# A decoder block in fp32: the up-projection by seven block products in place of eight, activations through DRAM

## The chip, the cores and the metric

The kernel runs on one core of a Trainium2 chip, as one program. The metric is the device time of one execution in microseconds (us). TensorE (PE) multiplies, VectorE (DVE), ScalarE (ACT) and GpSimd (POOL) work elementwise, SyncE (SP) issues the transfers between DRAM and SBUF. Accumulators stand in PSUM, eight banks of 128 x 512 fp32.

## The reference, cut to what matters

SEQ is 1024, D_MODEL 1024, D_FF 2816. The whole block is computed: modulation rows from c, two attention branches, their merge and w_out, the feed-forward part, a last norm. The part that the change touches:

```python
def conv_ffn(h, w_up, conv_w, conv_b, w_down):
    u = h @ w_up                                   # [1024, 2 * 2816]
    up = jnp.pad(u, ((0, 0), (CONV_WIDTH - 1, 0), (0, 0)))
    u = conv_b + sum(conv_w[j] * up[:, j:j + s] for j in range(CONV_WIDTH))
    gate, val = u[..., :D_FF], u[..., D_FF:]
    return (jax.nn.silu(gate) * val) @ w_down
...
    x = x + g_m[:, None, :] * mix                  # mix: the branches merged, times w_out
    h = modulate(rmsnorm(x, norm_ffn_g[l]), sh_f, sc_f)
    x = x + g_f[:, None, :] * conv_ffn(h, ...)
return rmsnorm(x, norm_final_g)
```

## The kernel before, in words

Every fp32 operand of a matmul is split into a high part (`hi_act`, a copy on ScalarE into the type fp32r, L75) and a low part (the operand minus its high part, `lo_dve` on VectorE, L84, or `lo_pool` on GpSimd, L87). One product of 128 x 128 by 128 x 512 is then three matmuls: high by high, high by low, low by high (`mm3`, L94 to L96).

The phases run one after the other: modulated input and projections, attention with the gate projections as fillers, then `mix_and_up`, `ffn_up` and `ffn_down`. A scheduler sets the order of instructions on each engine from the order of the code and the data that each needs; the loads go through one queue on SP, in order. Buffers come from pools: a name (tag) with a number of buffers that are used in turn, and whoever asks for the next one waits for the last reader of the old contents.

`mix_and_up` merges the branches (L962 to L975), then multiplies by w_out in four groups: two halves of the tokens times two halves of 512 columns, each with four accumulators. `load` and `scaled_rows` bring rows of w_out, scaled by the modulation row gm on GpSimd (L1069). `residual` adds x (L1001), `modulated` makes the norm of a token tile (L1009 on VectorE, L1010 on VectorE or for three tiles on GpSimd). The rows gm, gf and sf are made by `late_row` in the merging loop, each by a load of partial sums, a split, and four matmuls. `by_feature` transposes the normalised tiles on TensorE and splits them: h2[c], eight blocks of 128 features by 512 tokens, for two token chunks c.

`ffn_up` takes 22 blocks j of 128 columns, each with its gate columns and its value columns. `columns_of` loads 128 columns (512 KB, into a buffer of `wr`, a tag with two buffers) and splits them in halves by `halves`: high parts on ScalarE, low parts on GpSimd. Each block needs four accumulators (gate and value, two chunks) of 8 x 3 matmuls, 96 in all. `conv` reads the accumulators in PSUM: ScalarE makes the first tap with the bias (L1090), VectorE adds the other two (L1096), and short pieces of one or two tokens come from the earlier chunk. `gated` takes the sigmoid on ScalarE (L1105), multiplies by it on GpSimd (L1106) and by the value on VectorE (L1109). The 22 results stay in SBUF as `acts`.

`ffn_down` makes two passes of 512 columns over all 22 blocks, eight accumulators each: `split_act` splits an activation block, `scaled_rows` brings w_down scaled by a gain row. It loads the residual rows x2 in its first steps.

## Time and profile before

| what | value |
|---|---|
| time, median of 3 runs | 1697.14 us (1696.16 to 1700.38) |
| profiled execution: span from the first to the last instruction | 1692.6 us |
| the median's distance to this span | 4.5 us |
| matmuls in the profile | 7966 |
| ScalarE busy | 679.5 us (40%) |
| bytes moved by DMA | 197.74 MB, mean 117 GB/s |
| rows of w_up, loads | 44 of 512 KB |

The profiled execution has no time of its own beside its span; the runs were timed apart from it. A busy share is the time in which an engine had an instruction under way; a matmul's duration is longer than the distance between two starts, since matmuls are pipelined. "Idle before" is the time that an engine stood before instructions of a group, with what ended it.

### The profile page before, as it was taken

To read this page: it belongs to the slowest core of one execution; us is meant where nothing else is said; L and a number is where in the kernel's file an instruction comes from. 1 tells how busy PE (TensorE), PEld (TensorE's weight loads), DVE (VectorE), ACT (ScalarE), POOL (GpSimd) and SP (SyncE) were. 2 spreads that over 40 slices of the span, in tenths; PEclk is the share of its full clock that TensorE was granted. 3 is DMA by queue.
4 is the path that set the end of the run, shared out by engine and by line. 5 is a ranking of instruction groups with operands and counts; after the bars stand their busy time and mean duration, and the time that the engine had idled before them with its cause. 6 is when DMAs were issued, how large, how long until landed. Compare 5 with 4: busy or idle time off the path is not lost.

```text
span 1692.6 us, 21545 instructions
## 1 busy us (share of the span) xinstructions
PE 1640.9 (97%) x7966; PEld 1349.1 (80%) x7966; DVE 911.7 (54%) x1620; ACT 679.5 (40%) x1265; POOL 597.5 (35%) x490
## 2 busy tenths in 40 slices
PE   7999989999989999999999899999999999999997
...
PEclk9999999999989999999999999999999999999999
...
GB/s 291 128 113 165 176 257 194 201 201 180 153 179 86 119 123 99 108 127 268 126 99 175 106 50 50 50 50 51 50 51 49 41 48 64 154 50 38 50 50 100
DMA packets 160696, 197.74 MB, mean 117 GB/s; under 512 B 9698, under 2 KB 106658, under 8 KB 159246
## 3 DMA queue, kind: packets, MB, share of 16 engines
...
## 4 chain that ended last, share of the span: by engine, by line
PE 53%; DVE 3%; ACT 1%; DMA 1%; issue 0%; SPq 0%; ACTq 0%
PE ps_mm L95 17%; PE ps_mm L96 17%; PE ps_mm L94 17%; PE ps_tr L314 0%; DVE h2x_h L1009 0%; DMA o_raw<-dram_gate 0%; DMA o_raw<-dram_o 0%; DVE h2x_h L1010 0%; PE psA_pt L767 0%; DVE small_rstd L106 0%; PE psA_pt L96 0%; PE psA_pt L94 0%; PE psA_pt L95 0%; PE psA_s L738 0%; PE psA_o L779 0%
## 5 line engine op out<-in xcount | busy, mean ns | idle before, releaser
L87 POOL TENSOR_TENSOR ws_wl<-wr_wr,ws_wh 128x512 fp32r<-128x512 f32 x150 | 200.5, 1338 | 390.5 <-ACT ws_wh L75 351.2
L94 PE MATMUL ps_mm<-h_h,ws_wh 128*128 128x512 f32 x704 | 274.6, 390 | 0.0
L95 PE MATMUL ps_mm<-h_h,ws_wh 128*128 128x512 f32 x704 | 274.5, 390 | 0.0
L96 PE MATMUL ps_mm<-h_h,ws_wl 128*128 128x512 f32 x704 | 274.4, 390 | 0.0
L75 ACT ACTIVATE ws_wh<-wr_wr 128x512 fp32r<-128x512 f32 x226 | 142.1, 631 | 250.8 <-PE ps_mm L95 146.6
L1096 DVE SCALAR_TENSOR_TENSOR up_uv<-ps_mm,cw_cw,up_uv 128x511 f32<-128x511 f32 (+1 forms) x132 | 69.5, 568 | 163.8 <-ACT up_uv L1090 163.0
L95 PEld LDWEIGHTS ps_mm<-h_h,ws_wh 128*128 128x128 f32 x704 | 132.4, 188 | 27.9 <-DVE h_h L84 0.4
L96 PEld LDWEIGHTS ps_mm<-h_h,ws_wl 128*128 128x128 f32 x704 | 132.4, 188 | 27.5
L94 PEld LDWEIGHTS ps_mm<-h_h,ws_wh 128*128 128x128 f32 x704 | 132.4, 188 | 27.4
L94 PE MATMUL psA_fill<-hT_hi,ws_wh 128*128 128x512 f32 x352 | 150.0, 426 | 0.0
L96 PE MATMUL psA_fill<-hT_hi,ws_wl 128*128 128x512 f32 x352 | 139.4, 396 | 0.0
L95 PE MATMUL psA_fill<-hT_lo,ws_wh 128*128 128x512 f32 x352 | 139.3, 396 | 0.0
L1096 DVE SCALAR_TENSOR_TENSOR act_act<-ps_mm,cw_cw,act_act 128x511 f32<-128x511 f32 (+1 forms) x132 | 69.4, 568 | 122.2 <-ACT act_act L1090 121.4
L748 ACT ACTIVATE att_p<-psA_s,small_soft 128x128 f32<-128x128 f32 (+7 forms) x128 | 94.8, 740 | 99.9 <-DVE small_soft L742 98.4
L738 PE MATMUL psA_s<-opn_k,opn_q 96*128 96x256 f32 (+7 forms) x480 | 115.0, 360 | 13.8 <-DMA opn_k<-opn_stg 7.9
L742 DVE TENSOR_REDUCE small_soft<-psA_s 128x1 f32<-128x128 f32 (+7 forms) x128 | 96.0, 752 | 52.8 <-PE psA_s L740 52.4
L1106 POOL TENSOR_TENSOR act_act<-act_act,up_sg 128x512 f32<-128x512 f32 x44 | 56.7, 1289 | 158.9 <-ACT up_sg L1105 158.9
L84 DVE TENSOR_TENSOR ws_wl<-wr_wr,ws_wh 128x512 fp32r<-128x512 f32 x76 | 84.4, 1113 | 32.7 <-ACT ws_wh L75 32.5
L95 PE MATMUL ps_mm<-ws_wl,ahp_ah 128*128 128x512 f32 x256 | 101.5, 396 | 0.0
L94 PE MATMUL ps_mm<-ws_wh,ahp_ah 128*128 128x512 f32 x256 | 101.3, 396 | 0.0
L738 PEld LDWEIGHTS psA_s<-opn_k,opn_q 96*128 96x128 f32 (+1 forms) x480 | 82.5, 193 | 23.0 <-issue 13.4
L96 PE MATMUL ps_mm<-ws_wh,ahp_al 128*128 128x512 f32 x256 | 100.5, 393 | 0.0
...
## 6 DMA issues: line engine op xcount, KB each, us to landing
...
```

Source lines behind the costliest of these rows:

```text
L75: self.nc.scalar.activation(out, in_, AF.Copy, scale=scale)
L84: self.nc.vector.tensor_tensor(out=out, in0=in_, in1=f32(hi), op=ALU.subtract)
L87: self.nc.gpsimd.tensor_tensor(out=out, in0=in_, in1=f32(hi), op=ALU.subtract)
L94: mm(ps, lhsT=lh, rhs=rh, start=start, stop=False)
L95: mm(ps, lhsT=lh, rhs=rl, start=False, stop=False)
L96: mm(ps, lhsT=ll, rhs=rh, start=False, stop=stop)
L738: mm(o, lhsT=l, rhs=r[:, keys], start=n_ == 0, stop=diag is None and n_ == len(passes) - 1)
L742: nc.vector.tensor_reduce(out=st[:, 0:1], in_=view(s), axis=AX.X if i < 4 else AX.XY, op=ALU.max, negate=True)
L748: nc.scalar.activation(po, view(s), AF.Exp, bias=st[:, 0:1], accum_out=st[:, 1:2])
L1096: nc.vector.scalar_tensor_tensor(out=d, in0=src, scalar=cw[:, tap, jj : jj + 1], in1=d, op0=ALU.mult, op1=ALU.add)
L1106: nc.gpsimd.tensor_tensor(out=act, in0=act, in1=sg, op=ALU.mult)
```

## The change

**Seven products.** The feature axis (1024 = two halves of 512) and the token axis (two chunks of 512) of the right-hand side are taken as four blocks B11, B12, B21, B22; the gate and value columns of block j as A11, A12 (gate) and A21, A22 (value). Winograd's form of Strassen's scheme needs seven products of 4 x 3 matmuls: `product` with A11 B11, A12 B21, s1 N1, s2 T2, s3 N3, s4 B22 and A22 N4. The sums of weights s1 to s4 are made by four additions on VectorE for each block (`sums`, L1157 to L1160), and split; the sums of the right-hand side (N1, T2, N3, N4) are made once, in `second_chunk`, by token tile. B11 and B21 come from `first_chunk`. Three products are accumulated onto a bank that already holds another one, whose first value has been copied out (c1, c5, c7). GpSimd takes c7 - c5 (L1202), and VectorE combines the products (L1209, L1210, L1212, L1214) into ug and uv, 1024 tokens in SBUF.

**The convolution** reads ug and uv in SBUF, in one piece of 1024 tokens for each tap (L1174), so the short pieces at the chunk's border are gone. The low parts of w_up move from GpSimd to VectorE (`split`).

**Through DRAM.** Each activation block is stored to d_act (512 KB) and loaded again in each pass of `ffn_down`, into a tag of four buffers.

**Rows and buffers.** gm alone is made in the merging loop; gf and sf (rows 4 and 3) are made behind w_out's first group, from the four buffers of tag "x", which the loads of x use next. PSUM has one tag of eight banks. For the first four blocks the products with B11 and B21 are made between the token tiles of `second_chunk` (`begin_products`). The gain row of `ffn_down` and the buffers for its activations take memory that `ffn_up` used.

```diff
-            for late, g, row in ((1, 5, gf), (2, 2, gm), (4, 4, gf), (5, 3, sf)):
+            for late, g in ((1, 5), (3, 2)):
                 if d == late:
-                    self.late_row(g, op, row)
+                    self.late_row(g, op, gm)
                     if g == 5:
-                        self.dma(self.d_row, gf[0:1, :])
+                        self.dma(self.d_row, gm[0:1, :])
...
-        self.h2 = [[h2p([P, KD, 512], R32, f"h{c}{i}") for i in range(2)] for c in range(2)]
-        hx = Pool(tc, "h2x", "left")
+        b1 = [h2p([P, KD, 512], R32, f"b1{i}") for i in range(2)]
+        gx = Pool(tc, "gx", "right")
+        gf, sf = (gx([P, D], F32, n) for n in ("gf", "sf"))
+        raw = gx([P, KD, 512], F32, "raw")
         groups = [(half, slice(n * 512, (n + 1) * 512)) for half in range(2) for n in range(2)]
...
-        def by_feature(t, h):
-            self.to_feature_major(h, KD, *self.h2[t // 4], t % 4, ps)
+        def turned(t, h, b):
+            pt = ps([P, 512], F32, "mm", 8)
+            for k in range(4):
+                nc.tensor.transpose(pt[:, k * P : (k + 1) * P], h[:, (4 * b + k) * P : (4 * b + k + 1) * P], self.ident)
+            return pt.rearrange("p (k n) -> p k n", n=P)
+        def first_chunk(t, h):
+            for b in range(2):
+                v = turned(t, h, b)
+                sl = (slice(None), slice(4 * b, 4 * b + 4), slice(t * P, (t + 1) * P))
+                nc.scalar.activation(raw[sl], v, AF.Copy)
+                self.hi_act(b1[0][sl], v)
+                self.lo_dve(b1[1][sl], v, b1[0][sl])
...
-                    by_feature(i, hs[i])
+                    first_chunk(i, hs[i])
+            if g == 0:
+                self.late_row(4, gx, gf, "x")
+                self.late_row(3, gx, sf, "x")
             if g % 2 == 0:
                 for t in range(4 * half, 4 * half + 4):
-                    xs.append(xp([P, D], F32, "x", 4))
+                    xs.append(gx([P, D], F32, "x", 4))
                     self.dma(xs[-1], a["x"][0, t * P : (t + 1) * P, :])
...
-        units = []
-        for b in range(2):
-            units.append(self.up_product(first[b], 0))
-            for t in (4 + 2 * b, 5 + 2 * b):
-                by_feature(t, hs[t])
...
+        self.tp = tp = Pool(tc, "t", "left")
+        names = ("B22", "N1", "T2", "N3", "N4")
+        tt = {n: [tp([P, 4, 512], R32, f"{n}{i}") for i in range(2)] for n in names}
+        self.right = {n: [x[:, 4 * i : 4 * i + 4, :] for x in b1] for i, n in enumerate(("B11", "B21"))} | tt
+        def second_chunk(t, h):
+            b12, b22 = (turned(t, h, b) for b in range(2))
+            cs = slice((t - 4) * P, (t - 3) * P)
+            x, z = (gx([P, D], F32, "x", 4).rearrange("p (i k n) -> p i k n", i=2, n=P) for _ in range(2))
+            v = {"N1": x[:, 0], "T2": x[:, 1], "N3": z[:, 0], "N4": z[:, 1]}
+            V = nc.vector.tensor_tensor
+            nc.scalar.activation(v["N3"], b22, AF.Copy)
+            V(out=v["N1"], in0=raw[:, 0:4, cs], in1=b12, op=ALU.subtract)
+            V(out=v["T2"], in0=b22, in1=v["N1"], op=ALU.add)
+            V(out=v["N3"], in0=b12, in1=v["N3"], op=ALU.subtract)
+            nc.gpsimd.tensor_tensor(out=v["N4"], in0=raw[:, 4:8, cs], in1=v["T2"], op=ALU.subtract)
+            v["B22"] = b22
+            for n in names:
+                hi, lo = (y[:, :, cs] for y in tt[n])
+                self.hi_act(hi, v[n])
+                (self.lo_pool if n == "N4" else self.lo_dve)(lo, v[n], hi)
+        early = 4
+        first = []
+        for j in range(early):
+            first.append(self.begin_products(j))
+            second_chunk(4 + j, hs[4 + j])
+        gx.close()
+        self.ffn_up(first)
...
-    def conv(self, u, before, dst, jj):
...
+    def up_raw(self, j):
+        out = []
+        for b in range(2):
+            c0 = b * DFF + j * P
+            w = self.wr([P, 1024], F32, "wr", 2)
+            self.dma(w.rearrange("p (k n) -> p k n", n=P), self.a["w_up"][0, :, c0 : c0 + P].rearrange("(k p) n -> p k n", p=P))
+            out.append(w)
+        return out
+    def split(self, x):
+        hi, lo = self.ws([P, 512], R32, "wh", 4), self.ws([P, 512], R32, "wl", 4)
+        self.hi_act(hi, x)
+        self.lo_dve(lo, x, hi)
+        return hi, lo
+    def product(self, acc, left, right, first):
+        wh, wl = left
+        xh, xl = self.right[right]
+        for k in range(4):
+            ks = slice(k * P, (k + 1) * P)
+            self.mm3(acc, wh[:, ks], wl[:, ks], xh[:, k, :], xl[:, k, :], first and k == 0, first and k == 3, not first)
+    def begin_products(self, j):
+        g, v = self.up_raw(j)
+        a11, a12 = (self.split(g[:, i * 512 : (i + 1) * 512]) for i in range(2))
+        x1 = self.ps([P, 512], F32, "mm", 8)
+        self.product(x1, a11, "B11", True)
+        c1 = self.tp([P, 512], F32, "c1", 4)
+        self.nc.scalar.activation(c1, x1, AF.Copy)
+        self.product(x1, a12, "B21", False)
+        return x1, c1
+    def sums(self, g, v):
+        V = self.nc.vector.tensor_tensor
+        x, z = (self.uw([P, 1024], F32, "s", 2) for _ in range(2))
+        lo_half, hi_half = slice(0, 512), slice(512, 1024)
+        V(out=x[:, lo_half], in0=v[:, lo_half], in1=v[:, hi_half], op=ALU.add)
+        V(out=x[:, hi_half], in0=g[:, lo_half], in1=v[:, lo_half], op=ALU.add)
+        V(out=z[:, lo_half], in0=x[:, lo_half], in1=g[:, lo_half], op=ALU.add)
+        V(out=z[:, hi_half], in0=z[:, lo_half], in1=g[:, hi_half], op=ALU.add)
+        out = []
+        for s in (x, z):
+            hi, lo = self.uw([P, 1024], R32, "sh", 2), self.uw([P, 1024], R32, "sl", 2)
+            self.hi_act(hi, s)
+            self.lo_dve(lo, s, hi)
+            out += [(hi[:, h], lo[:, h]) for h in (lo_half, hi_half)]
+        return out[0], out[2], out[1], out[3]
+    def conv(self, u, dst, jj):
         nc, cw = self.nc, self.cw
         nc.scalar.activation(dst, u, AF.Identity, bias=cw[:, 3, jj : jj + 1], scale=cw[:, 2, jj : jj + 1])
         for tap, back in ((1, 1), (0, 2)):
...
+            nc.vector.scalar_tensor_tensor(out=dst[:, back:], in0=u[:, : S - back], scalar=cw[:, tap, jj : jj + 1], in1=dst[:, back:], op0=ALU.mult, op1=ALU.add)
+    def ffn_up(self, first):
+        nc, ps = self.nc, self.ps
+        self.uw = Pool(self.tc, "uw", "left")
+        self.up = up = Pool(self.tc, "up", "right")
+        V = nc.vector.tensor_tensor
+        c0, c1_ = slice(0, 512), slice(512, 1024)
         for j in range(NJ):
+            bank = lambda: ps([P, 512], F32, "mm", 8)
+            g, v = self.up_raw(j)
+            if j < len(first):
+                x1, c1 = first[j]
+            else:
+                a11, a12 = (self.split(g[:, i * 512 : (i + 1) * 512]) for i in range(2))
+                x1 = bank()
+                self.product(x1, a11, "B11", True)
+                c1 = self.tp([P, 512], F32, "c1", 4)
+                nc.scalar.activation(c1, x1, AF.Copy)
+            s1, s2, s3, s4 = self.sums(g, v)
+            a22 = self.split(v[:, 512:1024])
+            x5, x7 = bank(), bank()
+            self.product(x5, s1, "N1", True)
+            c5 = up([P, 512], F32, "c", 4)
+            nc.scalar.activation(c5, x5, AF.Copy)
+            self.product(x7, s3, "N3", True)
+            c7 = up([P, 512], F32, "c", 4)
+            nc.scalar.activation(c7, x7, AF.Copy)
+            nc.gpsimd.tensor_tensor(out=c7, in0=c7, in1=c5, op=ALU.subtract)
+            if j >= len(first):
+                self.product(x1, a12, "B21", False)
+            ug, uv = up([P, S], F32, "u", 5), up([P, S], F32, "u", 5)
+            nc.scalar.activation(ug[:, c0], x1, AF.Copy)
+            x6 = bank()
+            self.product(x6, s2, "T2", True)
+            V(out=c1, in0=x6, in1=c1, op=ALU.subtract)
+            V(out=uv[:, c1_], in0=c1, in1=c7, op=ALU.add)
+            self.product(x5, s4, "B22", False)
+            V(out=ug[:, c1_], in0=x5, in1=c1, op=ALU.subtract)
+            self.product(x7, a22, "N4", False)
+            V(out=uv[:, c0], in0=x7, in1=c1, op=ALU.add)
+            act, sg, vc = (up([P, S], F32, "u", 5) for _ in range(3))
+            self.conv(ug, act, j)
+            nc.scalar.activation(sg, act, AF.Sigmoid)
+            nc.gpsimd.tensor_tensor(out=act, in0=act, in1=sg, op=ALU.mult)
+            self.conv(uv, vc, NJ + j)
+            V(out=act, in0=act, in1=vc, op=ALU.mult)
+            self.dma(self.d_act[j], act)
...
-            self.hi_act(ah, self.acts[k])
-            self.lo_dve(al, self.acts[k], ah)
+            act = self.ahp([P, S], F32, "act", 4)
+            self.dma(act, self.d_act[k])
+            self.hi_act(ah, act)
+            self.lo_dve(al, act, ah)
```

The order of instructions on VectorE, in the middle of `ffn_up`. Names are the program's tile names with a number; `wr` is a loaded tile of w_up, `ws_wl` a low part, `uw_s` a sum of weights, `t_c` a copy c1, `up_u` one of ug, uv, act, sg and the value. Before:

```order
L1096 SCALAR_TENSOR_TENSOR act_act_11_9389<-ps_mm_10817,cw_cw_8445,act_act_11_9389 128x511
L1096 SCALAR_TENSOR_TENSOR act_act_11_9389<-ps_mm_10817,cw_cw_8445,act_act_11_9389 128x510
L1096 SCALAR_TENSOR_TENSOR up_uv_10873<-ps_mm_10842,cw_cw_8445,up_uv_10873 128x511
L1096 SCALAR_TENSOR_TENSOR up_uv_10873<-ps_mm_10842,cw_cw_8445,up_uv_10873 128x510
L1109 TENSOR_TENSOR act_act_11_9389<-act_act_11_9389,up_uv_10873 128x512
L1096 SCALAR_TENSOR_TENSOR act_act_11_9389<-ps_mm_10878,cw_cw_8445,act_act_11_9389 128x511
L1096 SCALAR_TENSOR_TENSOR act_act_11_9389<-ps_mm_10817,cw_cw_8445,act_act_11_9389 128x1
L1096 SCALAR_TENSOR_TENSOR act_act_11_9389<-ps_mm_10878,cw_cw_8445,act_act_11_9389 128x510
L1096 SCALAR_TENSOR_TENSOR act_act_11_9389<-ps_mm_10817,cw_cw_8445,act_act_11_9389 128x2
```

Now, from the last two taps of one block to the combinations of the next:

```order
L1174 SCALAR_TENSOR_TENSOR up_u_11147<-up_u_11102,cw_cw_8435,up_u_11147 128x1023
L1174 SCALAR_TENSOR_TENSOR up_u_11147<-up_u_11102,cw_cw_8435,up_u_11147 128x1022
L1220 TENSOR_TENSOR up_u_11145<-up_u_11145,up_u_11147 128x1024
L84 TENSOR_TENSOR uw_sl_11337<-uw_s_11330,uw_sh_11336 128x1024
L84 TENSOR_TENSOR ws_wl_11345<-wr_wr_11305,ws_wh_11344 128x512
L1209 TENSOR_TENSOR t_c_23_11183<-ps_mm_11249,t_c_23_11183 128x512
L1210 TENSOR_TENSOR up_u_11247<-t_c_23_11183,up_c_11231 128x512
L1157 TENSOR_TENSOR uw_s_11475<-wr_wr_11450 128x512
L1158 TENSOR_TENSOR uw_s_11475<-wr_wr_11448,wr_wr_11450 128x512
L1212 TENSOR_TENSOR up_u_11246<-ps_mm_11203,t_c_23_11183 128x512
L84 TENSOR_TENSOR uw_sl_11341<-uw_s_11331,uw_sh_11340 128x1024
```

Before, two taps of each accumulator and one product made up nearly all of the work, with PSUM tiles as the first input. Now the taps read `up_u`, and low parts (L84) and sums of the block after the next (L1157, L1158) stand between them. The last L84 reads wr_wr_11305, the value columns of one block, and three rows on L1157 reads wr_wr_11450, those of the next.

The order on SP's queue in the same stretch. Before:

```order
L72 DMA wr_wr_10807<-in_w_up_dram 128x8x128
L72 DMA wr_wr_10943<-in_w_up_dram 128x8x128
L72 DMA wr_wr_10953<-in_w_up_dram 128x8x128
L72 DMA wr_wr_11089<-in_w_up_dram 128x8x128
L72 DMA wr_wr_11099<-in_w_up_dram 128x8x128
```

Now:

```order
L72 DMA wr_wr_11013<-in_w_up_dram 128x8x128
L72 DMA dram_act_64_147<-up_u_10710 128x1024
L72 DMA wr_wr_11015<-in_w_up_dram 128x8x128
L72 DMA wr_wr_11158<-in_w_up_dram 128x8x128
L72 DMA dram_act_65_148<-up_u_10855 128x1024
L72 DMA wr_wr_11160<-in_w_up_dram 128x8x128
```

Before, the queue holds loads of w_up alone, one buffer after the other. Now a store of an activation block (dram_act) stands between the load of the gate columns and that of the value columns.

The order on SP's queue around the loads of x for the first half of the tokens. Before, in the merging loop:

```order
L72 DMA o_raw_7917<-dram_acc_46_129 128x1024
L72 DMA wr_wr_8102<-in_w_o_fox_dram 128x4x128
L72 DMA x_x_8623<-in_x_dram 128x1024
L72 DMA x_x_8625<-in_x_dram 128x1024
L72 DMA x_x_8627<-in_x_dram 128x1024
L72 DMA x_x_8629<-in_x_dram 128x1024
L72 DMA o_raw_7942<-dram_gate_19_102 128x1024
```

Now, in w_out's groups, where gx_x_8614 and gx_x_8628 are the partial sums of rows 4 and 3:

```order
L72 DMA gx_x_8614<-dram_acc_45_128 128x1024
L72 DMA gx_gf_8451<-in_norm_ffn_g_dram 128x1024
L72 DMA wr_wr_8578<-in_w_out_dram 128x2x512
L72 DMA gx_x_8628<-dram_acc_44_127 128x1024
L72 DMA wr_wr_8657<-in_w_out_dram 128x2x512
L72 DMA wr_wr_8693<-in_w_out_dram 128x2x512
L72 DMA gx_x_8641<-in_x_dram 128x1024
L72 DMA gx_x_8643<-in_x_dram 128x1024
L72 DMA gx_x_8645<-in_x_dram 128x1024
L72 DMA gx_x_8647<-in_x_dram 128x1024
L72 DMA wr_wr_8729<-in_w_out_dram 128x2x512
```

The four loads of x stood among the loads of the merging loop, ahead of all of w_out; now they stand behind seven of its loads and behind the partial sums, whose buffers they take over.

## Rows read from the trace of the kernel before

**Rows 1.** The page: the span, busy time of the engines, and TensorE's granted clock in tenths.

```profile
span 1692.6 us, 21545 instructions
...
PE 1640.9 (97%) x7966; PEld 1349.1 (80%) x7966; DVE 911.7 (54%) x1620; ACT 679.5 (40%) x1265; POOL 597.5 (35%) x490
...
PEclk9999999999989999999999999999999999999999
```

**Rows 2.** Stretches: busy time and instructions of each engine, clock, DMA share, 1000 to 1430 us.

```profile
core 0: us, PE busy (x) PEld busy (x) DVE busy (x) ACT busy (x) POOL busy (x), PEclk, DMA share, GB/s
...
1000.00:1430.00 430.00, 430.00 (x1899) 356.06 (x1898) 153.69 (x278) 130.87 (x199) 157.21 (x122) 1.00 0.17 49
```

**Rows 3.** Timeline of TensorE (start, length, engine, line); last, one line's matmuls with their starts.

```profile
947.38 0.40 PE L94 MATMUL ps_mm<-h_h,ws_wh 128*128 128x512 f32 x1
...
960.98 0.67 PE L314 MATMUL ps_tr<-const_ident,h2x_h 128*128 128x128 f32 x4 [3.66 <-DVE h_h L84]
...
961.88 0.63 PE L95 MATMUL ps_mm<-h_h,ws_wh 128*128 128x512 f32 x1
...
969.04 0.73 PE L94 MATMUL ps_mm<-h_h,ws_wh 128*128 128x512 f32 x2
...
1437.33 0.39 PE L94 MATMUL ps_mm<-ws_wh,ahp_ah 128*128 128x512 f32 x1
...
L94 PE MATMUL ps_mm<-h_h,ws_wh x704: 387/389/712, 947.4 to 1436.6; 128*128 128x512 f32 x176
```

**Rows 4.** Timeline of VectorE (DVE), 947 to 960 us: the last residuals and norms.

```profile
947.57 1.28 DVE L1009 SCALAR_TENSOR_TENSOR h2x_h<-x_x,small_rstd,x_gf 128x1024 f32<-128x1024 f32 x1
948.77 0.68 DVE L1001 TENSOR_TENSOR x_x<-ps_mm,x_x 128x512 f32<-128x512 f32 x1
949.37 1.72 DVE L1010 TENSOR_TENSOR h2x_h<-h2x_h,x_sf 128x1024 f32<-128x1024 f32 x1
...
952.48 0.16 DVE L106 SCALAR_TENSOR_TENSOR small_rstd<-small_rstd 128x1 f32<-128x1 f32 x1
...
954.07 2.39 DVE L106 SCALAR_TENSOR_TENSOR small_rstd<-small_rstd 128x1 f32<-128x1 f32 x1
...
957.82 1.22 DVE L1010 TENSOR_TENSOR h2x_h<-h2x_h,x_sf 128x1024 f32<-128x1024 f32 x1
958.96 1.28 DVE L1009 SCALAR_TENSOR_TENSOR h2x_h<-x_x,small_rstd,x_gf 128x1024 f32<-128x1024 f32 x1
```

**Rows 5.** GpSimd (POOL): a group of 1000 to 1430 us, and one instruction of the timeline.

```profile
L1106 POOL TENSOR_TENSOR act_act<-act_act,up_sg 128x512 f32<-128x512 f32 x40 | 51.6, 1289 | 128.7 <-ACT up_sg L1105 128.7
...
954.05 2.40 POOL L1010 TENSOR_TENSOR h2x_h<-h2x_h,x_sf 128x1024 f32<-128x1024 f32 x1 [1.81 <-DVE small_rstd L105]
```

**Rows 6.** Timeline, 1484 to 1493 us: a load of w_down, GpSimd's scaling, low parts on VectorE.

```profile
1484.34 0.69 DVE L84 TENSOR_TENSOR ws_wl<-wr_wr,ws_wh 128x512 fp32r<-128x512 f32 x1
...
1485.05 0.37 SPq L72 DMA_DIRECT2D wr_wr<-in_w_down_dram  x1
...
1488.66 3.54 POOL L1069 TENSOR_TENSOR wr_wr<-wr_wr,ahp_gf 128x512 f32<-128x512 f32 x2 [7.59 <-DMA wr_wr<-in_w_down_dram]
...
1488.80 2.25 DVE L84 TENSOR_TENSOR ahp_al<-act_act,ahp_ah 128x1024 fp32r<-128x1024 f32 x1 [3.77 <-ACT ahp_ah L75]
1490.97 1.78 DVE L84 TENSOR_TENSOR ws_wl<-wr_wr,ws_wh 128x512 fp32r<-128x512 f32 x1
```

**Rows 7.** VectorE by shape, 780 to 960 us: busy us, mean ns, idle before, releaser.

```profile
L84 DVE TENSOR_TENSOR ws_wl<-wr_wr,ws_wh 128x512 fp32r<-128x512 f32 x32 | 34.5, 1077 | 28.2 <-ACT ws_wh L75 28.1
L968 DVE TENSOR_TENSOR o_raw<-ps_mm,o_raw 128x512 f32<-128x512 f32 x24 | 16.3, 684 | 12.4 <-ACT o_raw L961 10.1 <-PE ps_mm L96 2.4
```

**Rows 8.** Timeline: a load of w_in on SP's queue and its reader on ScalarE.

```profile
208.22 0.40 SPq L72 DMA_DIRECT2D wr_wr<-in_w_in_dram  x1
...
212.49 1.06 ACT L75 ACTIVATE opn_q<-wr_wr 128x1024 fp32r<-128x1024 f32 x1 [2.37 <-DMA wr_wr<-in_w_in_dram]
```

**Rows 9.** Stretches of 1 us while a load of w_up lands; columns as in rows 2.

```profile
1006.00:1007.00 1.00, 1.00 (x6) 0.84 (x5) 0.00 (x0) 0.99 (x1) 0.00 (x0) 1.00 1.09 324
```

More of the change, by code (lines that the diff above doesn't have):

```diff
@@ L163, in scratch @@
         self.d_x1 = [d([P, D], F32, f"x1{k}") for k in range(NT)]
+        self.d_act = [d([P, S], F32, f"act{j}") for j in range(NJ)]
     def columns(self, st):
@@ L1091, in conv @@
         for tap, back in ((1, 1), (0, 2)):
-            parts = [(dst[:, back:], u[:, : 512 - back])]
-            if before is not None:
-                parts.append((dst[:, :back], before[:, 512 - back :]))
-            for d, src in parts:
-                nc.vector.scalar_tensor_tensor(out=d, in0=src, scalar=cw[:, tap, jj : jj + 1], in1=d, op0=ALU.mult, op1=ALU.add)
-    def gated(self, j, c, units, before):
-        nc = self.nc
-        act = self.acts[j][:, c * 512 : (c + 1) * 512]
-        g0, v0 = before or (None, None)
-        self.conv(units[0], g0, act, j)
-        sg = self.up([P, 512], F32, "sg", 1)
-        nc.scalar.activation(sg, act, AF.Sigmoid)
-        nc.gpsimd.tensor_tensor(out=act, in0=act, in1=sg, op=ALU.mult)
-        uv = self.up([P, 512], F32, "uv", 2)
-        self.conv(units[1], v0, uv, NJ + j)
-        nc.vector.tensor_tensor(out=act, in0=act, in1=uv, op=ALU.mult)
```

60 lines of the change are left out of this document (18 added, 42 removed).

## The prediction, before the change was run

> **What bounds the kernel now.** I read the page's busy shares first. TensorE is busy 97% of the span at a granted clock near full; VectorE is at 54% and GpSimd at 35% [rows 1]. Over the whole kernel only matmul work is worth removing. A share is an average, so the second view is the table by stretches, for the stage that the change rewrites: in 1000 to 1430 us TensorE is busy 430.00 of 430 us, VectorE 153.69, ScalarE 130.87, GpSimd 157.21 [rows 2]. So before the change this stage is limited by matmuls alone, and VectorE has 276 us of slack there. Third, TensorE's timeline: the up-projection's first matmul starts at 947.38, the uninterrupted run at 969.04, and the down-projection's first matmul at 1437.33 [rows 3]. There are 3 x 704 = 2112 matmuls of that kind (the row of one of the three lines stands in [rows 3]), 48 of them before 969.04. The pitch is (1437.33 - 969.04) / 2064 = 0.227 us, and the last up matmul is followed by the first down matmul with no gap.
>
> **What the change removes.** Seven products of 12 matmuls for each of 22 blocks in place of 96: 264 matmuls x 0.227 = 59.9 us. One block takes TensorE 84 x 0.227 = 19.05 us instead of 21.8. If nothing else bound, the kernel would gain most of the 60 us.
>
> **What it adds to VectorE.** One steady period of the new order on VectorE (one j) has 18 instructions: eleven over 512 elements (four combinations of products, four sums of weights, three low parts), three two-input ones over 1024 and four convolution taps over 1022 or 1023. Rows of before that stand back to back give the distance from start to start: 1.20 us for a scalar-and-tensor operation over 1024 (947.57 to 948.77), 0.60 for 512 (948.77 to 949.37), 1.14 for a tensor operation over 1024 (957.82 to 958.96) [rows 4]. So 11 x 0.60 + 3 x 1.14 + 4 x 1.20 = 14.8 us a period, where the old stage spent 153.69 / 430 x 21.8 = 7.8.
>
> **The term I think decides: GpSimd stops VectorE.** GpSimd runs two instructions per period, c7 - c5 over 512 (1.29 us, as the row of the same size) and act x sg over 1024 (2.40 us) [rows 5]. At 954.05 GpSimd started such a 1024 operation, and a VectorE instruction on one value per partition, which took 0.16 us at 952.48, started at 954.07 and ended with it, after 2.39 us [rows 4, 5]. At 1488.66 two GpSimd operations took 3.54 us; the two low parts on VectorE beside them took 2.25 and 1.78 against 1.22 and 0.69 alone [rows 4, 6]. Between 780 and 960 the low parts of weights, which read only SBUF, average 1.077 us, while the products with a PSUM input stay at 0.684 [rows 7]. In the old stage VectorE's main instructions read PSUM, and it waits most of the time anyway. In the new one the taps read ug and uv in SBUF, and so do sums and low parts: nearly all of the period can be stopped. I take the whole 1.29 + 2.40 = 3.7 us; the bounds are 0 (GpSimd always meets a PSUM read or an idle VectorE) and 3.7. The Trainium skill (SBUF — State Buffer, "Who interferes with whom") says that a VectorE instruction with two SBUF inputs contends with a GpSimd instruction that reads SBUF, and one with at most one SBUF input does not. The PSUM rows agree; by that rule alone the lock here lies nearer to 3.7 than to 0, since 15 of the 18 instructions have both inputs in SBUF.
>
> **The DMA wait.** wr keeps two buffers. v(j+3) can be issued only after the low part of a22(j+2), the last instruction of a period, and the first sum of the next period reads it two instructions (2 x 0.60 = 1.2 us) later. VectorE works in order, so everything behind that sum waits. A load of the same 512 KB from issue to its reader takes 1488.66 - 1485.05 = 3.6 us; with other traffic 212.49 - 208.22 = 4.27 [rows 6, 8]. The wait is 3.6 - 1.2 = 2.4 us a period, the quieter row being nearer to this stage; bounds 0.4 (only the 1.6 us that 512 KB take at 324 GB/s [rows 9]) and 3.1. The order has this shape from the fifth period to the twentieth, 15 times; in the earlier ones 5 to 18 instructions lie between, which cover it.
>
> So VectorE's period is 14.8 + 3.7 + 2.4 = 20.9 us against 19.05 of TensorE: **the stage becomes VectorE's**. Bounds: 19.05 (lock hidden, TensorE binds) to 22.
>
> **Before the stage.** The late rows g=4 and 3 and the loads of x now share four buffers of tag x. SP's loads of x wait for TensorE's reads of the late rows behind w_out's group 0, and group 1 needs banks that the residual frees. The loads then cost about 3.6 us plus the residual's 0.6 before TensorE goes on, where they used to be far ahead: 5 us, with 3 more for the eight matmuls and the slower clock after the stop. Bounds 0 and 12. So w_out ends at 955 instead of 947. Then VectorE's chain for the right-hand operands: 28 instructions of 512 (16.8 us), four of 1.20 and three of 1.14 for the norm (8.2), 16 small ones of 0.15 (2.4), seven low parts of weights (4.2), the sums and one low part of 1024 for block 0 (3.5): 35 us. GpSimd's share in it, one operation over 1024 and eight over 512 (N4 and its low part), is 2.40 + 8 x 1.29 = 12.7 in the same lock. 955 + 48 = 1003. The cover is small: the four early blocks' products are only 96 matmuls, 22 us. Bounds 990 (no lock) and 1010.
>
> **The sum.** From 1003, three products (36 x 0.227 = 8) to VectorE's first combination: 1011. The first five periods, with 10, 13, 14, 18 and 17 us of work, and 3.7 each: 90, so 1101. Fifteen periods of 20.9: 1415. The last block has no loads ahead: its low part, three products and then the last two, 17: TensorE ends the stage at 1432. The step into the down-projection was free [rows 3]. Now the gain row's load waits for the last read of B22, the splits of w_down queue on GpSimd behind act x sg of block 21, and acts 0 and 1 come back from DRAM: 3.6 for the load, or the chain of combination, copies, two taps, sigmoid (about 6) and 2.40, then 1.29, a high part and two low parts (4): about 14, and 2 for the slower clock after a stop. Bounds 8 and 20. The down stage starts at 1448. Its own length, 1692.6 - 1437.3 = 255.3 [rows 1, 3], I leave: its 44 loads of acts are 22 MB in 255 us, 90 GB/s, and a single load moved 324 GB/s; four buffers cover their trip. Storing acts is covered the same way. The new span is 1703 against 1692.6: 10.7 us longer. The median of the runs, 1697.1, is 4.5 above the profiled span; with that kept, 1708.
>
> **The rivals.** *TensorE stays the bound.* The lock meets PSUM reads and idle time, so the period falls to 19.05. Then 1003 + 1752 matmuls x 0.227 = 1400, plus 16 and 255: span 1672, time 1676, faster. For it: reads of PSUM are not slowed [rows 7], and one VectorE low part beside GpSimd lost 1.0 us, not the operation's whole length [rows 6]. Against it: the 2.39 us for one value per partition [rows 4], and the load's wait alone leaves only 1.9 us of lock that a period can hide. It decides where lock and load wait together are under 4.2 us. *Half the lock.* Period near 19.9, 15 us less: 1693, at the edge. A period of 20.2 is break-even. *TensorE also loses its clock.* Each period now has a stop of TensorE of up to 2 us. After the stop of 3.66 us that ended at 960.98 a matmul lasted 0.63 us in place of 0.39 (961.88 against 1437.33) [rows 3], and I count 4 us of this. If each period lost 1 to 2 us so, the period would be about 22: 15 to 20 us more, 1725. *The change does not do what it says*: the instruction order shows the 84 matmuls per block, so I give this nothing.
>
> **How the numbers follow.** The forecast (period 20.5 to 21.4) 0.42, TensorE bound 0.25, half the lock 0.15, clock or a longer transition 0.18. A measurement of this kernel can tell some 0.3% (5 us) from no change. Faster by more: all of the second and half of the third, 0.33. Within: the rest of the third and a quarter of the first, 0.17. Slower: 0.50. The range 1674 to 1730 leaves out the transition's lower bounds together with a stage bound by TensorE, and the upper half of the last case.
>
> **What would show it.** In the new trace: VectorE's busy share in the stage near 85 to 95%; act x sg with a tap or a low part beside it that is as long as it; the first sum of weights waiting 2 to 3 us for the load of w_up; stops of TensorE of about 2 us a period; the stage's last matmul near 1432 and the first down matmul some 14 us later. A stage with TensorE busy throughout and a last up matmul near 1400 would prove me wrong, and so would a VectorE that waits at the sums for nothing.

## The result, and the profile after

The changed kernel takes 1706.34 us (median of 5 runs, 1704.19 to 1715.42); the kernel before, run beside it, 1697.14 (1693.8 to 1700.38). The ratio is 1.0062 with a 95% interval of 1.0037 to 1.0087: **slower by 0.6%**, about 10 us, where 1708 was forecast. The page of the changed kernel:

```profile
span 1704.6 us, 21282 instructions
...
PE 1605.0 (94%) x7702; PEld 1307.5 (77%) x7702; DVE 1135.2 (67%) x1728; ACT 746.9 (44%) x1333; POOL 537.5 (32%) x410
...
PEclk9999979999999999999999899999999998999999
```

TensorE has 7966 - 7702 = 264 matmuls less than in [rows 1] and is busy for 36 us less, and still the span is 12 us longer: TensorE is busy 94% instead of 97%, VectorE 67% instead of 54%. The stretches (columns as in [rows 2]) say where it stands still:

```profile
960.00:1010.00 50.00, 37.72 (x144) 28.46 (x143) 43.20 (x55) 24.66 (x40) 14.48 (x9) 0.83 0.30 84
...
1100.00:1400.00 300.00, 280.36 (x1195) 225.12 (x1193) 251.96 (x257) 127.40 (x171) 65.64 (x28) 0.99 0.23 74
...
1420.00:1460.00 40.00, 25.32 (x94) 19.48 (x94) 23.83 (x19) 13.25 (x17) 16.95 (x9) 0.83 0.44 161
```

In 1100 to 1400 TensorE is busy 280 of 300 us and VectorE 252; in [rows 2] it was 430 of 430 with VectorE at 154 of 430. The other two rows are the ways into and out of the stage, each with a slow clock. VectorE's groups of 1100 to 1400 (count, busy us, mean ns, idle before and its releaser):

```profile
L1174 DVE SCALAR_TENSOR_TENSOR up_u<-up_u,cw_cw,up_u 128x1023 f32<-128x1023 f32 x29 | 58.5, 2016 | 7.8 <-ACT up_u L1172 7.8
L1174 DVE SCALAR_TENSOR_TENSOR up_u<-up_u,cw_cw,up_u 128x1022 f32<-128x1022 f32 x28 | 48.6, 1734 | 0.5
...
L84 DVE TENSOR_TENSOR ws_wl<-wr_wr,ws_wh 128x512 fp32r<-128x512 f32 x42 | 27.7, 685 | 0.0
...
L1157 DVE TENSOR_TENSOR uw_s<-wr_wr 128x512 f32<-128x512 f32 x14 | 9.7, 692 | 36.3 <-DMA wr_wr<-in_w_up_dram 36.3
```

A tap that takes 1.28 us alone (as the operation of the same form in [rows 4], and as the taps of e_silu below) takes 2.02 and 1.73 here, while the low parts keep the 0.69 of [rows 6]. L1157, the first sum of weights, waited 36.3 us for the load of w_up in all, 14 times. VectorE stands still for 48 of the 300 us: these 36.3, 7.8 for ScalarE's first tap, and gaps between instructions; no wait for a buffer or for GpSimd's product is among them. One period of the timeline, with GpSimd's and SP's rows:

```profile
1201.74 0.69 DVE L1209 TENSOR_TENSOR t_c<-ps_mm,t_c 128x512 f32<-128x512 f32 x1
...
1213.69 2.78 POOL L1218 TENSOR_TENSOR up_u<-up_u,up_u 128x1024 f32<-128x1024 f32 x1 [16.02 <-issue]
1216.74 1.95 POOL L1202 TENSOR_TENSOR up_c<-up_c,up_c 128x512 f32<-128x512 f32 x1 [0.27 <-ACT up_c L1201]
...
1214.72 5.06 DVE L1174 SCALAR_TENSOR_TENSOR up_u<-up_u,cw_cw,up_u 128x1023 f32<-128x1023 f32 x2 [0.52 <-ACT up_u L1172]
...
1222.76 0.69 DVE L1209 TENSOR_TENSOR t_c<-ps_mm,t_c 128x512 f32<-128x512 f32 x1
1223.55 0.69 DVE L1210 TENSOR_TENSOR up_u<-t_c,up_c 128x512 f32<-128x512 f32 x1
...
1222.87 0.37 SPq L72 DMA_DIRECT2D wr_wr<-in_w_up_dram  x1
...
1226.77 0.69 DVE L1157 TENSOR_TENSOR uw_s<-wr_wr 128x512 f32<-128x512 f32 x1 [2.52 <-DMA wr_wr<-in_w_up_dram]
```

From 1201.74 to 1222.76 is a period of 21.0 us. GpSimd's two instructions cover 1213.69 to 1218.69; the two value taps in that time take 5.06 us together, where 2.4 is their time alone. Then the load: the last low part ends at 1222.84, SP issues at 1222.87, and the sum that reads it starts at 1226.77, 3.9 us after the issue, having waited 2.52. TensorE in the same stage and at its end:

```profile
1125.47 0.80 PE L94 MATMUL ps_mm<-h_b,ws_wh 128*128 128x512 f32 x1 [2.07 <-ACT t_c L1192]
1126.06 0.63 PE L95 MATMUL ps_mm<-h_b,ws_wh 128*128 128x512 f32 x1
...
1231.59 0.50 PE L94 MATMUL ps_mm<-h_b,ws_wh 128*128 128x512 f32 x1 [1.58 <-ACT t_c L1192]
1231.93 0.40 PE L95 MATMUL ps_mm<-h_b,ws_wh 128*128 128x512 f32 x1
...
1446.31 0.79 PE L94 MATMUL ps_mm<-ws_wh,ahp_ah 128*128 128x512 f32 x1 [11.12 <-ACT ahp_ah L75]
1446.90 0.63 PE L95 MATMUL ps_mm<-ws_wl,ahp_ah 128*128 128x512 f32 x1
...
1451.42 1.21 PE L96 MATMUL ps_mm<-ws_wh,ahp_al 128*128 128x512 f32 x4 [1.44 <-DVE ahp_al L84]
```

In the stage TensorE stops in most periods, for 1.4 to 2.4 us. The trace names ScalarE's copy of c1 (L1192) as what ends the stop; that copy stands in ScalarE's queue behind the first tap of the gate (L1172), which waits for VectorE's L1212, which stands behind the waiting sum:

```profile
1228.78 1.24 ACT L1172 ACTIVATE up_u<-up_u,cw_cw 128x1024 f32<-128x1024 f32 x1 [8.91 <-DVE up_u L1212]
...
1230.97 0.57 ACT L1192 ACTIVATE t_c<-ps_mm 128x512 f32<-128x512 f32 x1
```

The phases ahead of the change differ from run to run: in two runs of one kernel (e_all and e_all5 below) the first up matmul starts at 957.6 and at 950.3. So beside the ratio I give the length from that matmul to the end of the span (from one trace of each kernel; two kernels that were traced twice gave 717.9 and 718.0, and 714.0 and 714.1): before 1692.6 - 947.4 = 745.2 us; after, with the row

```profile
L94 PE MATMUL ps_mm<-h_b,ws_wh x176: 387/389/795, 949.6 to 1426.0; 128*128 128x512 f32 x176
```

1704.6 - 949.6 = 755.0.

### The profile page after: what moved, and what is told of

It reads as the page before. It is cut to its first block, busy times and chain, and to the rows that moved or that the text cites. A ratio compares the mean times of both kernels' runs of the same rounds, so it can differ in the third digit from the quotient of the medians.

```text
span 1704.6 us, 21282 instructions
## 1 busy us (share of the span) xinstructions
PE 1605.0 (94%) x7702; PEld 1307.5 (77%) x7702; DVE 1135.2 (67%) x1728; ACT 746.9 (44%) x1333; POOL 537.5 (32%) x410
## 5 line engine op out<-in xcount | busy, mean ns | idle before, releaser
L1174 DVE SCALAR_TENSOR_TENSOR up_u<-up_u,cw_cw,up_u 128x1023 f32<-128x1023 f32 x88 | 163.6, 1859 | 18.4 <-ACT up_u L1172 17.9
L1218 POOL TENSOR_TENSOR up_u<-up_u,up_u 128x1024 f32<-128x1024 f32 x22 | 61.4, 2791 | 327.7 <-issue 296.5
L87 POOL TENSOR_TENSOR ws_wl<-wr_wr,ws_wh 128x512 fp32r<-128x512 f32 x62 | 83.3, 1345 | 229.6 <-ACT ws_wh L75 199.1
L84 DVE TENSOR_TENSOR ws_wl<-wr_wr,ws_wh 128x512 fp32r<-128x512 f32 x142 | 126.4, 904 | 25.0 <-ACT ws_wh L75 24.9
L1172 ACT ACTIVATE up_u<-up_u,cw_cw 128x1024 f32<-128x1024 f32 x44 | 54.4, 1237 | 153.9 <-DVE up_u L1212 153.8
L94 PE MATMUL ps_mm<-ws_wh,ahp_ah 128*128 128x512 f32 x256 | 101.5, 396 | 11.1 <-ACT ahp_ah L75 11.1
L84 DVE TENSOR_TENSOR ahp_al<-ahp_act,ahp_ah 128x1024 fp32r<-128x1024 f32 x32 | 42.8, 1340 | 88.7 <-ACT ahp_ah L75 88.7
L94 PE MATMUL ps_mm<-h_b,ws_wh 128*128 128x512 f32 x176 | 74.0, 420 | 27.5 <-ACT t_c L1192 24.4
L84 DVE TENSOR_TENSOR att_ptl<-psA_pt,att_pth 128x512 fp32r<-128x512 f32 x96 | 66.0, 688 | 33.4 <-ACT att_pth L75 33.1
L751 DVE TENSOR_SCALAR att_p<-att_p,small_soft 128x128 f32<-128x128 f32 (+7 forms) x128 | 84.4, 660 | 4.1
L768 PE MATMUL psA_pt<-const_ident,att_p 128*128 128x128 f32 x576 | 87.0, 274 | 0.0
```

The lines of the kernel that those rows point to most:

```text
L84: self.nc.vector.tensor_tensor(out=out, in0=in_, in1=f32(hi), op=ALU.subtract)
L87: self.nc.gpsimd.tensor_tensor(out=out, in0=in_, in1=f32(hi), op=ALU.subtract)
L94: mm(ps, lhsT=lh, rhs=rh, start=start, stop=False, skip_group_check=onto)
L751: nc.vector.tensor_scalar(out=pr, in0=pr, scalar1=st[:, 2:3], scalar2=None, op0=ALU.mult)
L768: nc.tensor.transpose(pt[:, n * 256 + e * P : n * 256 + (e + 1) * P], pr[:, kb * P : (kb + 1) * P], self.ident)
L1174: nc.vector.scalar_tensor_tensor(out=dst[:, back:], in0=u[:, : S - back], scalar=cw[:, tap, jj : jj + 1], in1=dst[:, back:], op0=ALU.mult, ...
```

## The experiments

All kernels start from the changed one. "Period" is the mean distance between starts of the first combination of products, over 15 blocks; 19.3 stands where it settles, at 19.27 to 19.29 for 12 blocks or more. e_v2 gets there in its last blocks only, after some of 18.85 to 19.1. e_noload computes something else than the block, since it leaves 43 loads out.

| run | ratio to the kernel before, 95% interval | first up matmul to the end, us | period, us |
|---|---|---|---|
| the change | 1.0062 (1.0037 to 1.0087) | 755.0 | 21.3 |
| e_v2 | 0.9895 (0.987 to 0.992) | 726.9 | 19.1 |
| e_silu | 0.9842 (0.9822 to 0.9862) | 717.8 | 19.3 |
| e_both, e_both5 | 0.9809 (0.9787 to 0.9831), 0.9843 (0.983 to 0.9857) | 717.9, 718.0 | 19.3 |
| e_gain | 1.0024 (1.0008 to 1.004) | 752.9 | 21.5 (its last 23.3) |
| e_lopool | 1.0109 (1.008 to 1.0137) | 763.7 | 21.5 |
| e_n4 | 1.0052 (1.0034 to 1.007) | 754.2 | 21.4 |
| e_noload | one run, 1707.4 us | 754.6 | 21.3 |
| e_early2 | 1.0107 (1.0093 to 1.0122) | 760.7 | 21.2 |
| e_bg | 0.984 (0.9826 to 0.9853) | 713.5 | 19.3 |
| e_all, e_all5 | 0.9831 (0.9799 to 0.9863), 0.9826 (0.9812 to 0.984) | 714.0, 714.1 | 19.3 |

**The load's wait (e_v2).**

```diff
-            w = self.wr([P, 1024], F32, "wr", 2)
+            w = self.wr([P, 1024], F32, "wr", 2) if b or not self.own_g else self.uw([P, 1024], F32, "g", 1)
```

> Gate columns get a buffer of their own (4 KB), so that the value columns alternate between the two of wr and their load no longer waits for the last instruction of a VectorE period. Theory 1 (VectorE is a chain: 14.8 us of work, 2.7 of stops by GpSimd, 2.5 of waiting for the load, 0.6 for ScalarE, some 0.5 of gaps make the period of 21.1): the load wait goes, VectorE comes to 18.6, TensorE binds at 19.05 to 19.4, and 15 periods give back 26 to 31 us: 1675 to 1681. Theory 2 (the stop that the trace names on TensorE, the copy c1 behind ScalarE's queue, is the limit by itself): the period stays within 0.3 us of 21.1, the time within 5 us of 1706. Theory 3 (more buffers only move the wait to the gate's load): period 20 to 21, 1690 to 1705.

The period fell to 19.1 and the length by 28 us, as theory 1 has it; the time, 1682.5 us, lies 1.5 above its range. TensorE's stops are gone with an edit that touches neither ScalarE nor its queue, so theory 2 falls, although the trace had named ScalarE. The stretch 1110 to 1400 and a period of VectorE:

```profile
1110.00:1400.00 290.00, 290.00 (x1265) 237.22 (x1264) 268.60 (x266) 136.06 (x176) 73.31 (x30) 1.00 0.25 81
...
1227.40 0.68 DVE L1211 TENSOR_TENSOR t_c<-ps_mm,t_c 128x512 f32<-128x512 f32 x1
...
1236.33 2.95 DVE L1175 SCALAR_TENSOR_TENSOR up_u<-up_u,cw_cw,up_u 128x1023 f32<-128x1023 f32 x1 [0.39 <-ACT up_u L1173]
...
1244.69 0.69 DVE L1158 TENSOR_TENSOR uw_s<-wr_wr 128x512 f32<-128x512 f32 x1
...
1246.50 0.68 DVE L1211 TENSOR_TENSOR t_c<-ps_mm,t_c 128x512 f32<-128x512 f32 x1
```

TensorE is busy 290 of 290 us. The tap beside GpSimd is still stopped (2.95), and no sum waits.

**GpSimd's stop (e_silu).**

```diff
-            nc.scalar.activation(sg, act, AF.Sigmoid)
-            nc.gpsimd.tensor_tensor(out=act, in0=act, in1=sg, op=ALU.mult)
+            nc.scalar.activation(act, act, AF.Silu)
```

> Sigmoid on ScalarE and the product with it on GpSimd become one Silu on ScalarE, so GpSimd keeps only c7 - c5 in each period; the buffers and the load wait stay. Theory 1: the pair of value taps takes 2.4 to 3.7 us instead of 5.06, the period 19.1 to 20.0, and 21 periods and the step into the down-projection (GpSimd's 2.3 us are gone there) give 22 to 40 us: 1666 to 1684. Theory 2: GpSimd is not on ScalarE's way; no change beyond 5 us from 1706. Theory 3 (GpSimd waits for VectorE rather than the other way, so the taps are long for their own reason): the taps stay at 5 us and the period at 21.

The taps of 1100 to 1400, and what GpSimd has left there:

```profile
L1174 DVE SCALAR_TENSOR_TENSOR up_u<-up_u,cw_cw,up_u 128x1022 f32<-128x1022 f32 x32 | 40.8, 1275 | 0.0
L1174 DVE SCALAR_TENSOR_TENSOR up_u<-up_u,cw_cw,up_u 128x1023 f32<-128x1023 f32 x31 | 39.6, 1278 | 0.1
...
L1202 POOL TENSOR_TENSOR up_c<-up_c,up_c 128x512 f32<-128x512 f32 x16 | 41.7, 2604 | 260.4 <-ACT up_c L1201 181.5 <-DVE ws_wl L84 44.7 <-DVE up_u L1219 34.2
```

All taps are back at 1.28 us and the period is 19.3: theory 1, and theory 3 falls. (The edit also takes one buffer of `up_u` less in each block; VectorE waited for none in the changed kernel, as its idle time there shows.) What I had not expected is in the last row: c7 - c5 takes 2.60 us, where such an operation takes 1.29 [rows 5]. It no longer runs beside the taps; it starts behind them, beside the product L1219 and low parts:

```profile
1141.49 1.22 DVE L1219 TENSOR_TENSOR up_u<-up_u,up_u 128x1024 f32<-128x1024 f32 x1
1141.59 4.00 POOL L1202 TENSOR_TENSOR up_c<-up_c,up_c 128x512 f32<-128x512 f32 x1 [14.18 <-DVE ws_wl L84]
1142.62 1.22 DVE L84 TENSOR_TENSOR uw_sl<-uw_s,uw_sh 128x1024 fp32r<-128x1024 f32 x1
1143.76 0.68 DVE L84 TENSOR_TENSOR ws_wl<-wr_wr,ws_wh 128x512 fp32r<-128x512 f32 x1
```

GpSimd was held up for as long as these three took, and none of them lost time. In other periods of this run a low part that starts while c7 - c5 is under way takes 1.02 or 1.23 us in place of 0.69, in time that VectorE has to spare. The Trainium skill (SBUF — State Buffer, "Who interferes with whom") says that issue order decides who blocks. These rows differ: by the start times of the trace both low parts came behind c7 - c5, and both went ahead of it. In the changed kernel the second value tap came behind c7 - c5 as well, and there the tap waited. What decides between the two isn't shown. The load's trip is not covered: the first sum still waited 21.7 us for it in 1100 to 1400, 1.5 us a period. But VectorE has that time now, since it also waited 26.7 us for TensorE's products at L1209.

**Both (e_both, e_both5).**

> Both edits at once: own buffer for the gate columns, and Silu without GpSimd. Theory 1: VectorE comes to about 17, TensorE binds at 19.05 to 19.3, the same period as with the buffer alone; the time 1670 to 1678, within 6 us of the buffer alone and no sum of the two gains. Theory 2: still 21 us a period. If the two gains add up (1640 to 1655), TensorE is not the next bound at 19.05.

> The same kernel as with both edits (own buffer, Silu), again beside the next two, since the phases ahead of the change differ by some us from run to run. 1666 to 1671; from the first up matmul to the end 717 to 719 us.

```profile
1110.00:1400.00 290.00, 290.00 (x1266) 237.16 (x1265) 239.02 (x263) 139.41 (x176) 27.14 (x15) 1.00 0.26 78
```

Busy 290 of 290 again, and the period settles at 19.3 as with each edit alone: the gains do not add up, TensorE binds. Over GpSimd's edit alone the buffer brings nothing (717.9 against 717.8). So neither wait alone made the stage VectorE's; it took the two together. One part of the expectation missed: the time is 15 us under that of the buffer alone (1667.81 and 1682.5), the length 9. These lie ahead of the steady blocks: the first seven periods take 127.7 us with the buffer alone and 116.6 with both.

**A part undone (e_lopool).**

```diff
-                a11, a12 = (self.split(g[:, i * 512 : (i + 1) * 512]) for i in range(2))
+                a11, a12 = (self.split(g[:, i * 512 : (i + 1) * 512], self.lo_pool) for i in range(2))
```

> One part of the change undone: the low parts of A11 and A12 go back to GpSimd from the fifth block on; all else stays. They are 2 x 0.6 us less for VectorE and 2 x 1.3 us more for GpSimd in each period. If GpSimd's instructions stop VectorE's for their whole length (theory 1), the period goes from 21.1 to 21.1 - 1.2 + 2.6 = 22.5 where none of it falls into VectorE's wait for the load, and to 19.9 where all of it does: I expect 21.5 to 22.5 and 1711 to 1727. If GpSimd is free help, as it was in the kernel before (rival), the period is 19.9 and the time 1685 to 1690.

The time is inside theory 1's range, the length 9 us more. VectorE got 1.2 us of work less in each period, and the period rose by 0.3. The sum L1160 of VectorE, 0.69 before, and the moved low parts on GpSimd:

```profile
L1160 DVE TENSOR_TENSOR uw_s<-uw_s,wr_wr 128x512 f32<-128x512 f32 x14 | 24.9, 1779 | 0.0
...
L87 POOL TENSOR_TENSOR ws_wl<-wr_wr,ws_wh 128x512 fp32r<-128x512 f32 x28 | 62.7, 2257 | 169.4 <-ACT ws_wh L75 157.5 <-PE ps_mm L95 11.9
```

A sum of 0.69 us takes 1.78 and a low part on GpSimd 2.26 instead of 1.3: each stops the other. The help that cost no time in the kernel before, where TensorE was busy 430 of 430 us [rows 2], costs time here.

**The step between the stages (e_gain).**

```diff
+        self.gain0 = self.cwp([P, 512], F32, "gf")
+        self.dma(self.gain0, self.d_row[:, 0:512].to_broadcast([P, 512]))
         for j in range(NJ):
...
+            if j == NJ - 1:
+                self.down0 = self.scaled_rows(self.a["w_down"], 0, c0, self.gain0)
```

> The gain row of the down-projection is loaded ahead of the up-projection into memory of its own, and the first two blocks of w_down are scaled and split ahead of the last block's sigmoid product; the loads of activations stay as they are. Theory 1 for the step between the stages (gain row, then GpSimd's queue, then the splits): TensorE's stop of 11.1 us at 1446 falls to 2 to 5, the time to 1697 to 1701. Rival (the activations coming back from DRAM set the stop): the stop stays at 8 to 11 and the time within 3 us of 1706.

TensorE's last two stops (the second is the first down matmul), and a low part of VectorE beside GpSimd's scaling:

```profile
1412.92 2.31 DVE L84 TENSOR_TENSOR uw_sl<-uw_s,uw_sh 128x1024 fp32r<-128x1024 f32 x1
...
1426.63 0.76 PE L94 MATMUL ps_mm<-h_b,ws_wh 128*128 128x512 f32 x1 [4.73 <-ACT t_c L1194]
...
1445.19 0.79 PE L94 MATMUL ps_mm<-ws_wh,ahp_ah 128*128 128x512 f32 x1 [5.65 <-ACT ahp_ah L75]
```

The stop of 11.12 us fell to 5.65, but a stop of 4.73 us appeared in the block before, where the changed kernel had 2.12: the scaling on GpSimd (a low part of 1.22 us takes 2.31 beside it) and the splits now stand in the way of a stage that VectorE limits. About 2 us of length remain of the gain, with some 6 us in the ratio. The time, 1703.44 us, missed theory 1's range and would fit the rival's; the stop decides against the rival, since it was halved with the activations' way left as it was. Where TensorE limits the stage, nothing is given back (e_bg: both edits and this one):

> Both edits and the early gain row, N4 left on GpSimd. TensorE binds the last blocks here, so none of the gain is given back in the blocks before, as it was with the gain row alone: 4 to 6 us from TensorE's shorter stop, 1661 to 1665, 712 to 714 us from the first up matmul to the end. If the early splits of w_down slow the last blocks again, 1666 to 1670.

The first down matmul of e_both5, then e_bg:

```profile
1409.45 0.79 PE L94 MATMUL ps_mm<-ws_wh,ahp_ah 128*128 128x512 f32 x1 [9.56 <-ACT ahp_ah L75]
```

```profile
1402.86 0.79 PE L94 MATMUL ps_mm<-ws_wh,ahp_ah 128*128 128x512 f32 x1 [4.52 <-ACT ahp_ah L75]
...
1406.34 1.22 PE L96 MATMUL ps_mm<-ws_wh,ahp_al 128*128 128x512 f32 x2 [0.98 <-DVE ahp_al L84]
```

The stop fell by 5.0 us and the length by 4.5 against e_both5, run beside it; the two traces of e_all, which has this edit too, agree (714.0 and 714.1 against 717.8 to 718.0 without it). In the ratios e_bg and e_both5 cannot be told apart (0.984 and 0.9843), and the time, 1669.64 us, lies in the range that I gave to the rival.

**N4 on VectorE (e_n4), and everything together (e_all, e_all5).**

```diff
-            nc.gpsimd.tensor_tensor(out=v["N4"], in0=raw[:, 4:8, cs], in1=v["T2"], op=ALU.subtract)
+            V(out=v["N4"], in0=raw[:, 4:8, cs], in1=v["T2"], op=ALU.subtract)
...
-                (self.lo_pool if n == "N4" else self.lo_dve)(lo, v[n], hi)
+                self.lo_dve(lo, v[n], hi)
```

> N4 and its low part, made in four token tiles ahead of the up-projection, go from GpSimd to VectorE: 8 x 0.60 = 4.8 us more work there, 8 x 1.3 = 10.4 us fewer stops. Theory 1: VectorE's chain between the last residual and the first combination is 4 to 6 us shorter, the time 1700 to 1702. Rival (GpSimd works beside VectorE there): 4.8 us longer, 1711.

> All that helped, together: own buffer for the gate columns, Silu on ScalarE, the gain row and the first blocks of w_down early, N4 on VectorE. TensorE binds the up-projection at 19.28 us a block, so the gains outside of it add up: from 1668 some 5 for N4 and 5 to 7 for the step between the stages, 1654 to 1660. If TensorE's stops between the stages come from the activations' way through DRAM, only N4's share comes: 1662 to 1665.

> All four edits again beside the two above. The stretch from the first up matmul to the end was 714.0 us in the run before; if N4 on VectorE is worth nothing, it is that of both edits with the gain row, within 2 us.

N4 was a miss: 754.2 against 755.0, and 1707.63 us fits neither range. My reading is that work and stops weigh about the same there, so that 1.3 us of stop for each of the eight was too much; the stops were not counted. In all edits together it brings nothing either (714.1 against 713.5 for e_bg). e_all missed as well: 1670.91 us where 1654 to 1660 was expected, or 1662 to 1665 by the other account. It has no gain from N4, 4 us from the step, and in the traced run its first up matmul came 8 us later than in the changed kernel. Measured side by side, e_bg and e_all5 take 1669.64 and 1667.34 us, the kernel before 1697.32: 1.6 to 1.7% faster than it, and by the ratios 2.2 to 2.3% faster than the change as it stands; by the ratios alone they cannot be told from e_both and e_both5.

**Through DRAM (e_noload).**

> The down-projection loads one activation block once and uses it for all 22 (the other 43 loads are left out); the stores to DRAM stay. My theory: the loads are covered, and the down-projection's 258.3 us are 3 longer than before for the slower clock and one low part at its start. Then its length from the first matmul on stays 257 to 259 us. Rival (44 loads of 512 KB delay w_down or the splits): it falls to 255.

The down-projection of the changed kernel, then of this one:

```profile
1446.00:1700.00 254.00, 248.59 (x1056) 198.88 (x1056) 125.23 (x160) 86.23 (x134) 76.57 (x50) 0.99 0.45 159
```

```profile
1447.00:1700.00 253.00, 248.53 (x1056) 198.88 (x1056) 139.17 (x156) 85.83 (x133) 85.35 (x50) 0.99 0.22 76
```

The DMA traffic halves (159 to 76 GB/s), TensorE's busy time does not move, and the stage lasts 1705.6 - 1447.5 = 258.1 us against 1704.6 - 1446.3 = 258.3. The loads are covered.

**Early products (e_early2).**

```diff
         for j in range(early):
-            first.append(self.begin_products(j))
+            if j < 2:
+                first.append(self.begin_products(j))
```

> Only the first two blocks' products with B11 and B21 are made between the token tiles, not four: 48 matmuls (10.9 us of TensorE) move from the stretch ahead of the up-projection into it. VectorE's work is the same. If VectorE's chain sets the time from the last residual to the last block (theory 1), TensorE takes them up in its stops of some 2 us a period, and the time stays within 4 us of 1706. If TensorE's work counts there (rival), it is 8 to 11 us longer: 1714 to 1717.

The rival's time (1715.17 us), and my expectation missed; the length grew by 5.7 us, about half of the 10.9 of matmuls that were moved. TensorE's first main product and the stretch behind it:

```profile
990.91 0.80 PE L94 MATMUL ps_mm<-t_N,uw_sh 128*128 128x512 f32 x1 [20.37 <-ACT uw_sh L75]
...
990.00:1048.00 58.00, 57.09 (x239) 46.45 (x240) 47.82 (x53) 26.87 (x34) 12.18 (x5) 0.95 0.31 91
```

TensorE waits 20.4 us for the sums to be ready and then works 57.1 of 58 us without a stop. My theory of VectorE's chain holds for the blocks with the load's wait; in the first blocks TensorE is nearly filled (53.55 us busy of 993 to 1050 in the changed kernel), so matmuls taken out of the gap ahead of them do cost time there.

## Why the prediction was right, point by point

- **The bound moves to VectorE: right**, shown by e_v2, e_silu and e_lopool. Forecast 20.9 us a period, measured 319.1 / 15 = 21.3 (combinations at 1093.83 and 1412.92). *Work* of 14.8 was taken from back-to-back rows and stands. *GpSimd's stop*, 3.7 forecast: the 57 taps of 1100 to 1400 took 107.1 us where 1.28 each is 73.0, so 34 us over some 14 periods, 2.4; in the period shown it is 5.06 - 2.40 = 2.7. That the price was the whole of GpSimd's time was the step that failed; VectorE loses what overlaps, and GpSimd loses as well (2.78 us for 2.40, 1.95 for 1.29). *The load*, 2.4 forecast: 36.3 / 14 = 2.6, since the trip was 3.9 us, not 3.6; the store of an activation block is issued 1.7 us ahead of the load, and whether it is what lengthens the trip wasn't tried. *Not in the sum*: value taps waiting for ScalarE's first tap, 7.8 / 14 = 0.6, and some gaps of 0.1 behind dependent instructions, 0.6 a period. So the period from 1222.76 to 1243.87, 21.1 us, is 14.8 of work, 2.7 of stop, 2.5 of load, 0.5 for ScalarE and 0.6 of gaps; some longer periods make the mean 21.3. The period was met in part by luck: 1.0 too much for the stop stands against 1.1 that the sum did not have.
- **Ahead of the stage: 7 us too long.** The first combination came at 1004.4, not 1011. The wait for x was the step that failed: it put w_out's end at 955, and the last residual came at 950.4. 5 us and 3 more were forecast, and TensorE did not stop at that place at all, and by the code four of the eight banks are free for the next group; it had one stop of 4.2 us later, for a low part of w_out, where the kernel before had one of 3.1. VectorE's chain, 48 us with its stops, took 43 (950.4 to 993.2), so it was 5 too long. Against both, the first three products took 11.3 us (993.1 to 1004.4), not 8; TensorE's granted clock in 960 to 1010 was 0.83.
- **The first five periods**: 90 forecast, 1093.8 - 1004.4 = 89.4 measured; but e_early2 shows that TensorE's work has its part there.
- **The last block: 5 us too short** (17 forecast, 22 from 1412.9 to the last matmul's end at 1435). **The step between the stages: 5 us too long** (16 forecast, a stop of 11.1), with the right mechanism, as e_gain shows. **The down-projection: 3 us too short**: some seven of its first matmuls took 0.63 us each (half clock), and one low part cost 1.4.
- The measured terms less the forecast ones are -6.6, -0.6 (the first five periods), +5.1 (the fifteen: 319.1 and 314), +5.3, -4.9 and +3.0. They sum to +1.3, and the span of 1704.6 is 1.6 over the forecast 1703: the time was met because the terms' errors cancel, which is luck. The 4.5 us that I put on top of the span were the spread of the runs; a run's time stands 1.7 us above its own span here (1706.34 and 1704.6).
- **The rivals.** TensorE as the bound is what the kernel becomes when either wait is taken away (e_v2, e_silu). The period then is 19.3, not 19.05. "Half the lock" was mispriced: by the prediction's own terms it is 14.8 + 1.85 + 2.4 = 19.05, TensorE's bound, and not 19.9. The clock: behind the stop of 2.07 us that ended at 1125.47 the granted clock was 0.50, behind the stop of 2.20 us that ended at 1041.90 it was 1.00 (columns as in [rows 2]):

```profile
1126.06:1128.62 2.56, 2.56 (x7) 1.98 (x6) 2.56 (x5) 1.15 (x2) 0.00 (x0) 0.50 0.00 0
...
1042.00:1044.00 2.00, 2.00 (x9) 1.66 (x10) 2.00 (x3) 0.42 (x1) 0.00 (x0) 1.00 0.86 246
```

From 1100 to the stage's end three stops have slow matmuls behind them (2.07, 2.37 and 2.12 us), some seven each. That rival is seen in a few periods only, and cost little: seven matmuls at 0.43 us from start to start in place of 0.23 are 1.4 us.

The account of the 59.9 us: the length from the first up matmul to the end grew by 9.8, so 70 us were lost. TensorE's stops and slow matmuls from the first combination to the last product are 430.8 us less the 1716 matmuls x 0.227 left there (389.5): 41 us. Some 4 of these are no stop: where TensorE binds, 84 matmuls take 19.28 us, 0.2295 each. The rest lies ahead (about 14 more than before), in the step (11) and behind it (3).
